# First norm of a hybrid block on one core: the weights as a scale of the evictions, two tiles turned by a diagonal, two turned plainly at another place

## The chip, the cores and the metric

The kernel runs on one core of a Trainium2 chip. The metric is the device time of one execution in microseconds, as the median of several runs. The core has five engines with queues of their own: PE (matrix products; its weight loads are listed as PEld), ACT (functions, with a scale and a bias per partition), DVE (element by element), POOL and SP. Data lie in 128 partitions; PE writes to PSUM banks of 128 x 512 f32 values, and ACT and DVE read them from there.

## The reference

512 tokens and 16 meta tokens in front of them (528 rows of 1024 values) pass a block: a norm over the row, a wide projection, a recurrent branch (convolution of 4 taps, two gates, a scan), a retention branch with four heads, their gated sum, and a feed-forward part with a convolution. The part that matters here is the first norm and the start of the recurrent branch:

```python
def rms_norm(x, g):
    x32 = x.astype(jnp.float32)
    y = x32 * lax.rsqrt(jnp.mean(x32 * x32, axis=-1, keepdims=True) + EPS)
    return (y * g.astype(jnp.float32)).astype(x.dtype)
...
h = jnp.concatenate([meta, x], axis=1)
xn = rms_norm(h, norm_mix_g[l])
z = xn @ w_in[l]
u_rnn, u_gate, q, k, v, g_ret, ga, gb = jnp.split(z, IN_SPLITS, axis=-1)
xr = causal_dwconv(u_rnn, rnn_conv_w[l], rnn_conv_b[l])
...
r = jax.nn.sigmoid(jnp.einsum('btni,nij->btnj', xb, w_a).reshape(bsz, t, D_RNN) + b_a)
i = jax.nn.sigmoid(jnp.einsum('btni,nij->btnj', xb, w_x).reshape(bsz, t, D_RNN) + b_x)
```

A row is divided by its root mean square, which is one number per token, and multiplied by a weight, which is one number per column.

## The kernel before

**Precision.** Every f32 operand of a product is split into a high and a low f16 part: ACT writes the high part (`split`, L91), DVE the rest (L92). A product of two operands takes three f16 products (high by high, high by low, low by high). The split normalized tokens are the tiles xh and xl, with the 1024 columns as 8 blocks of 128 partitions and the tokens along the free axis. Weights come by SP's queue into one of two raw buffers (`unit_load`, 1 MB or 0.5 MB a unit) and are split in steps into tiles wt; a raw buffer is free for the next load when DVE has done the last step of its unit.

**The first norm.** Tokens come as four tiles of 128 rows, two in each tile xin. For each tile ACT sums the squares (`rms_scale`, L320) and takes the root, DVE the reciprocal rs, and DVE multiplies the rows by rs and by the weights, which were read from memory into all 128 partitions (tile gmix, 512 KB, L402). PE turns the result by eight transposes into two PSUM banks (L411), and ACT and DVE split them into xh and xl, 512 columns at a time. The 16 meta tokens go a way of their own in the tile xmeta (L440 to L452). In between PE runs matmuls on zeros, `keep_warm` (L426), 18, 2, 5 and 6 of them.

**The first blocks.** The recurrent branch has ten blocks of 128 columns. The product of a block is done in two halves of tokens of 24 products each; the first half reads the meta tokens and tiles 0 and 1. `first_half` (L383) does the first halves of blocks 0, 1 and 2 as soon as these two tiles are split; tiles 2 and 3 are normed and turned meanwhile. Then the loop over the ten blocks starts: the second halves of blocks 0 to 2, from block 3 on whole blocks (48 products, L370); the convolution as a scaled copy on ACT (L537) and three taps on DVE (L539); the split of the result (tile xs); and three blocks later (LAG) the two gate products, with sigmoids on ACT (L556). `tick` emits weight steps of coming units between. The gate weights a and x are loaded into raw buffers by `load_gates` and split by `split_gates` (tiles gw), a behind the product of block 0, x behind that of block 2.

**Order.** From the first norm to the end of the recurrent branch, the orders of PE, ACT and DVE are those in which the program is written (`manual_schedule`); loads by `load` are kept in their written order on SP's queue. Each engine works in order: an instruction that waits holds those behind it.

Of the kernel before, what the change touches and what calls it, by code (L numbers as in the profile page):

```python
# [14 lines left out]
P = 128  # L15
T = 528
# [34 lines left out]
def hybrid_block_kernel(ctx, tc, x, meta, norm_mix_g, w_in, conv_w, conv_b, rg_a_w, rg_a_b,  # L51
# [44 lines left out]
    def load(dst, src):  # L96

        if last_load[0] is None:
            last_load[0] = nc.sync.dma_start(dst, src)
        else:  # L100
            with tc.issue_after(last_load[0].ins):
                last_load[0] = nc.sync.dma_start(dst, src)
# [7 lines left out]
    def unit(nk, ncol, parts, fast=False):  # L110
        units.append((nk, ncol, parts, fast))
        return len(units) - 1

    o_ur, o_ug, o_q, o_k, o_v, o_gr, o_ga, o_gb = 0, 1280, 2560, 3584, 4608, 6656, 8704, 9728
    u_ur = []
    for n in range(2):
        u_ur.append((unit(8, P, [(0, 0, kmaj(w_in, 0, 8, o_ur + P * n, P))]), 0))
    for i in range(1, 5):
        u = unit(8, 256, [(0, 0, kmaj(w_in, 0, 8, o_ur + 256 * i, 256))])
        u_ur += [(u, 0), (u, P)]  # L120
    u_ug = [unit(8, 256, [(0, 0, kmaj(w_in, 0, 8, o_ug + 256 * i, 256))]) for i in range(5)]
# [138 lines left out]
    def queue(new):  # L260
        steps.extend((len(loaded) - 1, run) for run in new)
# [52 lines left out]
    def pair(name):  # L314
        return [piece([P, 512], F32, f"{name}{a}") for a in range(2)]
# [79 lines left out]
    def token_rows(i):  # L395
        return xin[i // 2][:, i % 2]

    def first_rows(i, rs):
        xn_t[i] = pair("xn")
        for a in range(2):  # L400
            sl = slice(a * 512, (a + 1) * 512)
            nc.vector.scalar_tensor_tensor(xn_t[i][a], token_rows(i)[:, sl], rs, gmix[:, sl], op0=ALU.mult, op1=ALU.mult)  # L402

    def first_transpose(i, banks):
        xn = xn_t.pop(i)
        c0 = 3 + NM + P * i
        pvs = []
        for a in range(2):
            pv = banks[a].rearrange("p (b c) -> p b c", c=P)
            for k in range(4):  # L410
                nc.tensor.transpose(pv[:, k], xn[a][:, k * P:(k + 1) * P], ident)  # L411
            pvs.append(pv)

        def finish(*half):
            for a in half:
                sl = slice(4 * a, 4 * a + 4)
                split(xh[:, sl, c0:c0 + P], xl[:, sl, c0:c0 + P], pvs[a], S_XN)
        return finish

    warm = work.tile([P, 512], F16, name="warm", tag="w")  # L420
    nc.vector.memset(warm, 0.0)
# [12 lines left out]
    pmeta = acc("pmeta")[:, 0]
    xm, gm = xmeta[:, 0:P], xmeta[0:8, P:2 * P]
    first_rows(0, rms_scale(token_rows(0), P, "n"))
    finish0 = first_transpose(0, ptr_banks())
    first_rows(1, rms_scale(token_rows(1), P, "n"))
    ssm = small.tile([P, 4], F32, name="ssm")
    nc.scalar.activation(xmeta[:, 2 * P:3 * P], xm, AF.Square, accum_out=ssm[:, 0:1])  # L440
    nc.tensor.matmul(pmeta[:, 0:P], pick[0:8, 0:P], gm, start=True, stop=True)
    nc.tensor.matmul(pmeta[:, 2 * P:2 * P + 1], same[:, 0:P], ssm[:, 0:1], start=True, stop=True)
    finish0(0)
    finish0(1)
    keep_warm(2)
    pt1 = acc("pt1")
    finish1 = first_transpose(1, [pt1[:, 0], pt1[:, 1]])
    nc.scalar.activation(ssm[:, 1:2], pmeta[:, 2 * P:2 * P + 1], AF.Sqrt, scale=1.0 / D, bias=eps_t)
    nc.vector.reciprocal(ssm[:, 2:3], ssm[:, 1:2])
    nc.vector.scalar_tensor_tensor(xm, xm, ssm[:, 2:3], pmeta[:, 0:P], op0=ALU.mult, op1=ALU.mult)  # L450
    keep_warm(5)
    nc.tensor.transpose(pmeta[:, P:2 * P], xm, ident)  # L452
    keep_warm(6)
    def first_step():
        steps[done[0]][1]()
        done[0] += 1

    first_step()
    finish1(0)
    split(xh[:, :, 3:3 + NM], xl[:, :, 3:3 + NM], pmeta[:, P:2 * P].rearrange("p (t c) -> p c t", c=8), S_XN)  # L460
    first_step()
    finish1(1)
    first_rows(2, rms_scale(token_rows(2), P, "n"))
    first_half(0)
    for i in range(2):
        first_step()
    finish2 = first_transpose(2, ptr_banks())
    rs3 = rms_scale(token_rows(3), P, "n")
    finish2(0, 1)
    first_rows(3, rs3)  # L470
# [218 lines left out]
    nc.sync.dma_start(dec_meta, decay_t[:, :, T:].rearrange("h p c -> p h c"))  # L689
# [721 lines left out]
```

## Time and profile before

| | us |
|---|---|
| median of 3 runs (1078.16 to 1082.24) | 1078.28 |
| the profiled execution | 1080.82 |
| its span | 1079.1 |
| PE busy | 1059.0 |
| DVE busy | 839.4 |
| ACT busy | 568.2 |
| PE, first product that counts (L383) starts | 17.68 |
| PE, second half of block 0 starts | 28.68 |

The profile is one execution. Times in it count from the start of its span. A row of the timeline has the start, the busy time, the engine, the line, the operation, what it writes and reads, the shapes and the number of instructions; in brackets is the idle time of the engine before it and what ended it. A row of the chain of waits has start, length and what ran. A row of windows has the stretch, its length, the busy time and count of PE, PEld, DVE, ACT and POOL, then the granted clock of PE, the share of the DMA engines and GB/s. A DMA row has the queue, the count, the size and the time from issue to landing. Where a row has "x2" for one f32 product, these are its two passes.

### The profile page before, as it was taken

To read this page: it belongs to the slowest core of one execution; us is meant where nothing else is said; L and a number is where in the kernel's file an instruction comes from. 1 tells how busy PE (TensorE), PEld (TensorE's weight loads), DVE (VectorE), ACT (ScalarE), POOL (GpSimd) and SP (SyncE) were. 2 spreads that over 40 slices of the span, in tenths; PEclk is the share of its full clock that TensorE was granted. 3 is DMA by queue.
4 is the path that set the end of the run, shared out by engine and by line. 5 is a ranking of instruction groups with operands and counts; after the bars stand their busy time and mean duration, and the time that the engine had idled before them with its cause. 6 is when DMAs were issued, how large, how long until landed. Compare 5 with 4: busy or idle time off the path is not lost.

```text
span 1079.1 us, 20969 instructions
## 1 busy us (share of the span) xinstructions
PE 1059.0 (98%) x9045; PEld 856.6 (79%) x9045; DVE 839.4 (78%) x1220; ACT 568.2 (53%) x847; POOL 6.9 (1%) x20
## 2 busy tenths in 40 slices
PE   8999999999999999999999999999999999999997
PEld 5888888875684858888888885588888888888885
DVE  5875699998786969888697785478767776888875
ACT  6568963534564747566454453364544454454442
POOL 2000000000000000000000000000000000000000
PEclk9999999999999999999999999999999999999999
DMA  6423243431211311433333355053232323113322
GB/s 209 143 92 104 79 138 118 157 119 40 75 45 50 108 64 65 125 91 118 104 103 118 118 199 173 2 196 115 81 118 80 118 79 118 40 60 121 115 79 79
DMA packets 105957, 112.02 MB, mean 104 GB/s; under 512 B 3470, under 2 KB 97396, under 8 KB 105864
## 3 DMA queue, kind: packets, MB, share of 16 engines
q1 hardware_dynamic: 105432, 110.27, 31.1%
q8 instruction: 71, 1.16, 0.4%
q10 hardware_dynamic: 144, 0.26, 0.1%
q14 instruction: 22, 0.18, 0.1%
q0 software_dynamic: 288, 0.14, 0.0%
HBM read 108.57 MB, written 2.10 MB: 103 GB/s over the span
## 4 chain that ended last, share of the span: by engine, by line
PE 71%; DVE 17%; ACT 8%; issue 2%; DMA 2%; SPq 0%; ACTq 0%; DVEq 0%
PE ps L370 33%; PE P L1247 9%; PE pa L775 7%; DVE wt L92 4%; PE ps L838 4%; PE pm L370 4%; PE ps L1119 3%; PE ps L383 3%; PE pe L775 3%; ACT wt L91 2%; PE pb L775 2%; PE ps L860 1%; DVE rnn L574 1%; DVE raw L231 1%; DMA raw<-in_w_out 1%
## 5 line engine op out<-in xcount | busy, mean ns | idle before, releaser
L370 PEld LDWEIGHTS <-wt 128*128 128x128 f16 x4224 | 410.5, 97 | 63.7 <-DVE t L666 1.4
L92 DVE SCALAR_TENSOR_TENSOR wt<-raw,wt 128x1024 f16<-128x1024 f32 (+2 forms) x270 | 296.2, 1110 | 71.7 <-ACT wt L91 69.8
L91 ACT ACTIVATE wt<-raw 128x1024 f16<-128x1024 f32 (+2 forms) x270 | 256.1, 964 | 161.3 <-PE ps L370 28.3
L775 PEld LDWEIGHTS <-wt 128*128 128x128 f16 x2016 | 195.0, 97 | 36.0 <-issue 8.8
L370 PE MATMUL ps<-x2h,wt 128*128 128x258 f16 x1440 | 218.8, 273 | 0.0
L370 PE MATMUL ps<-xh,wt 128*128 128x257 f16 (+2 forms) x1056 | 163.8, 275 | 1.1 <-DVE t L666 1.1
L370 PE MATMUL ps<-x2l,wt 128*128 128x258 f16 x720 | 137.7, 272 | 0.0
L1204 DVE SCALAR_TENSOR_TENSOR cv<-ps,vt,cv 128x512 f32<-128x512 f32 x96 | 71.9, 748 | 54.5 <-ACT cv L1202 53.2
L370 PE MATMUL ps<-xl,wt 128*128 128x257 f16 (+2 forms) x528 | 102.2, 275 | 0.0
L1247 PE MATMUL P<-wt,act 128*128 128x256 f16 x792 | 88.3, 273 | 0.0
L1247 PEld LDWEIGHTS <-act 128*128 128x128 f16 x792 | 77.5, 98 | 9.0
L838 PE MATMUL ps<-wt,xh 128*128 128x512 f16 x256 | 76.4, 379 | 1.2 <-DVE v L92 1.0
L775 PE MATMUL pa<-xs,wt 128*128 128x257 f16 x576 | 71.6, 273 | 4.8 <-ACT kept L780 4.5
L1202 ACT ACTIVATE cv<-ps,vt,vt 128x512 f32<-128x512 f32 x48 | 37.1, 774 | 56.8 <-PE ps L370 52.2
L370 PE MATMUL pm<-oa,wt 128*128 128x257 f16 x480 | 55.4, 274 | 0.0
L838 PEld LDWEIGHTS <-xh 128*128 128x128 f16 x256 | 24.8, 98 | 30.9 <-issue 2.9
L838 PE MATMUL ps<-wt,xl 128*128 128x512 f16 x128 | 48.5, 379 | 0.0
L775 PE MATMUL pa<-ob,wt 128*128 128x257 f16 x384 | 45.7, 274 | 0.6 <-ACT last L780 0.5
L1119 PE MATMUL ps<-wt,mx 128*128 128x512 f16 x192 | 44.8, 379 | 0.5 <-DVE mx L92 0.5
L231 DVE TENSOR_TENSOR raw<-raw 128x1024 f32<-128x1024 f32 x35 | 42.7, 1220 | 0.6
L1119 PEld LDWEIGHTS <-mx 128*128 128x128 f16 x192 | 17.4, 98 | 19.2 <-DVE mx L92 1.0
L860 PE MATMUL ps<-sc,v 128*128 128x257 f16 (+4 forms) x384 | 32.1, 236 | 0.0
(253 smaller groups left out, 1278.1 us busy)
## 6 DMA issues: line engine op xcount, KB each, us to landing
raw<-in_w_in SPq DMA_DIRECT2D x41, 1024.0 KB, 4.9
raw<-in_w_up SPq DMA_DIRECT2D x24, 1024.0 KB, 5.0
raw<-in_w_down SPq DMA_DIRECT2D x48, 256.0 KB, 3.6
raw<-in_w_branch_ret SPq DMA_DIRECT2D x16, 512.0 KB, 4.0
raw<-in_w_branch_rnn SPq DMA_DIRECT2D x8, 640.0 KB, 4.2
raw<-in_w_out SPq DMA_DIRECT2D x4, 1024.0 KB, 4.9
xin<-in_x SPq DMA_DIRECT2D x4, 512.0 KB, 6.6
h<-in_x SPq DMA_DIRECT2D x4, 512.0 KB, 4.9
```

What stands on the lines that cost most here:

```text
L91: nc.scalar.activation(hi, src, AF.Copy, scale=s)
L92: nc.vector.scalar_tensor_tensor(lo, src, s, hi, op0=ALU.mult, op1=ALU.subtract)
L231: nc.vector.tensor_tensor(pair, pair, rv[:, :, right].rearrange("p (h k) c -> p h k c", h=2), op=ALU.add)
L370: nc.tensor.matmul(ps[:, hf, :n], w(aw, k, col, P), src(ax, k, c0, n), start=k == 0 and (aw, ax) == (0, 0), stop=k == nk - 1 and aw == 1)
L383: nc.tensor.matmul(ps[:, hf, :n], w(aw, k, col, P), src(ax, k, c0, n), start=k == 0 and (aw, ax) == (0, 0), stop=k == KD - 1 and aw == 1)
L775: nc.tensor.matmul(ps[:, :257], ws[k // 4](wf, aw, k % 4), src(xf_, ax, k), start=first and k == 0 and (aw, ax) == (0, 0), stop=k == last_ ...
L838: nc.tensor.matmul(pb, xf(ax, k, XF + j0, nb), w(aw, k % 4, 0, 512), start=i == 0, stop=i == 23)
L860: nc.tensor.matmul(ps[:, hf, s0 - lo_i:257], vt[b][:, va, d * P:(d + 1) * P], st[SCP[b][0]][:, sa, o:o + hi_i - s0], start=i == 0, stop=i ...
L1119: nc.tensor.matmul(ps[:, n], mx[k][:, a, c0:c0 + P], wo[k // 2](aw, k % 2, n * 512, 512), start=j == 0, stop=j == 23)
L1202: nc.scalar.activation(vv_, ps[:, :, 2:258], AF.Identity, scale=vt2[:, 96 + ch:97 + ch], bias=b_ff[:, ch:ch + 1])
L1204: nc.vector.scalar_tensor_tensor(vv_, ps[:, :, j:j + 256], vt2[:, 48 * j + ch:48 * j + ch + 1], vv_, op0=ALU.mult, op1=ALU.add)
L1247: nc.tensor.matmul(pd[:, 256 * tt:256 * tt + 256], t[:, ax, c0 + tt * P:c0 + tt * P + P], w(wf, aw, i), start=q % 6 == 0 and tt == 0 and i ...
```

## The change

1. **Weights as a scale.** The broadcast tile gmix goes. The 1024 weights come as 8 rows of 128 into xmeta (a load that was there for the meta tokens; now it is issued from ACT's queue), are turned by one small transpose and kept, times S_XN, as gs: one column of 128 values per block of columns. ACT and DVE multiply by a column of gs when they split, so each 128 x 512 eviction becomes four of 128 x 128.
2. **Tiles 0 and 1** are turned without being scaled first: `first_scale` makes a diagonal of the reciprocals, dg, and the turning is a product of the token rows with dg in f32 instead of a transpose of scaled rows.
3. **Tiles 2 and 3** are scaled by rs alone and transposed as before. Tile 3 goes into the free second halves of the banks of blocks 0 and 1, and stands behind the first half of block 2 instead of ahead of it.
4. **Loads.** The first two blocks' weights, two units of 128 columns, become one unit of 256, like the next, both loaded and split column by column (`column_unit`). The load of dec_meta leaves the head of SP's queue.
5. **Warming** is 15, 4 and 5 matmuls.
6. **Gates and steps.** Block 0 is split and the x gates are split earlier, behind blocks 0 and 1, and the weight steps of blocks 0 and 1 stand behind blocks 2 and 3.

```diff
-    for n in range(2):
-        u_ur.append((unit(8, P, [(0, 0, kmaj(w_in, 0, 8, o_ur + P * n, P))]), 0))
-    for i in range(1, 5):
+    for i in range(5):
...
+    def column_unit():
...
+        def fetch(c):
+            load(rv[:, :, c * P:c * P + P], ap[:, :, c * P:c * P + P])
...
+                split(tv[0], tv[1], rv[:, 4 * i:4 * i + 4, c * P:c * P + P], SW)
...
+        queue([step(i, c) for c in range(2) for i in range(2)])
...
-    gmix = wsp.tile([P, D], F32, name="gmix", tag="wt")
...
+    nc.scalar.dma_start(xmeta[0:8, P:2 * P], norm_mix_g.rearrange("(c f) -> c f", f=P))
     load(xin[0][:, 0], x2[0:P])
     load(xin[0][:, 1], x2[P:2 * P])
-    load(gmix, norm_mix_g.partition_broadcast(P))
     load(xmeta[:, 0:P], meta.rearrange("t (c f) -> (t c) f", f=P))
-    load(xmeta[0:8, P:2 * P], norm_mix_g.rearrange("(c f) -> c f", f=P))
...
+    def first_scale(i):
+        rs = rms_scale(token_rows(i), P, "n")
+        dg = piece([P, 512], F32, "dg")[:, 0:P]
+        nc.vector.tensor_scalar_mul(dg, ident, rs)
+        return dg
...
-            nc.vector.scalar_tensor_tensor(xn_t[i][a], token_rows(i)[:, sl], rs, gmix[:, sl], op0=ALU.mult, op1=ALU.mult)
+            nc.vector.tensor_scalar_mul(xn[a], token_rows(i)[:, 512 * a:512 * a + 512], rs)
...
+        def turn(a):
             for k in range(4):
-                nc.tensor.transpose(pv[:, k], xn[a][:, k * P:(k + 1) * P], ident)
+                c = 512 * a + k * P
+                if dg is None:
+                    nc.tensor.transpose(pvs[a][:, k], xn[a][:, k * P:k * P + P], ident)
+                else:
+                    nc.tensor.matmul(pvs[a][:, k], token_rows(i)[:, c:c + P], dg, start=True, stop=True)
+        def high(a):
+            for k in range(4):
+                g = gs[:, 4 * a + k:4 * a + k + 1]
+                nc.scalar.activation(xh[:, 4 * a + k, c0:c0 + P], pvs[a][:, k], AF.Copy, scale=g)
+        def low(a):
+            for k in range(4):
+                g = gs[:, 4 * a + k:4 * a + k + 1]
+                nc.vector.scalar_tensor_tensor(xl[:, 4 * a + k, c0:c0 + P], pvs[a][:, k], g,
+                                               xh[:, 4 * a + k, c0:c0 + P], op0=ALU.mult, op1=ALU.subtract)
...
-    keep_warm(18)
+    keep_warm(15)
...
+    nc.tensor.transpose(pmeta[:, 3 * P:3 * P + 8], gm, ident[0:8, 0:8])
+    nc.vector.tensor_scalar_mul(gs, pmeta[:, 3 * P:3 * P + 8], S_XN)
...
-    finish3 = first_transpose(3, ptr_banks())
     first_half(2)
...
+    turn3, high3, low3 = first_transpose(3, [early[i][:, 1] for i in range(2)], xn=xn3)
...
-            tick(2 if n in (6, 8) else 1)
+            tick(2 if n in (3, 6, 8) else 1)
...
-        if n < 2:
+        if n == 0:
+            conv_split(0)
+        if n == 1:
+            split_gates("x")
+        if n == 2:
             tick()
-        if n == 2:
-            conv_split(0)
-            split_gates("x")
...
-    nc.sync.dma_start(dec_meta, decay_t[:, :, T:].rearrange("h p c -> p h c"))
+    load(dec_meta, decay_t[:, :, T:].rearrange("h p c -> p h c"))
```

Three places show how the instructions move; lines are those of each kernel.

DVE from the first reciprocal, before (xn are the scaled rows, xin the token tiles):

```order
L324 RECIPROCAL rs<-sd 128x1
L402 SCALAR_TENSOR_TENSOR xn_154<-xin_110,rs,gmix 128x512
L402 SCALAR_TENSOR_TENSOR xn_155<-xin_110,rs,gmix 128x512
L324 RECIPROCAL rs<-sd 128x1
L402 SCALAR_TENSOR_TENSOR xn_175<-xin_110,rs,gmix 128x512
L402 SCALAR_TENSOR_TENSOR xn_176<-xin_110,rs,gmix 128x512
L92 SCALAR_TENSOR_TENSOR xl<-ptr,xh 128x4x128 x2
```

and now:

```order
L345 RECIPROCAL rs<-sd 128x1
L428 TENSOR_SCALAR dg<-ident,rs 128x128
L490 TENSOR_SCALAR gs<-pmeta 128x8
L345 RECIPROCAL rs<-sd 128x1
L428 TENSOR_SCALAR dg<-ident,rs 128x128
L461 SCALAR_TENSOR_TENSOR xl<-ptr,gs,xh 128x128 x8
```

The four scaled rows of 512 columns give way to two diagonals, and the two low parts of 512 columns to eight of 128.

PE at tile 3 (xn_287 and xn_288), before; first halves of blocks are the L383 rows:

```order
L411 MATMUL ptr<-ident,xn_287 128x128 x4
L411 MATMUL ptr<-ident,xn_288 128x128 x4
L383 LDWEIGHTS wt
L383 MATMUL ps<-xh,wt 128x267
L383 LDWEIGHTS wt
L383 MATMUL ps<-xl,wt 128x267
```

and now (xn_353 and xn_354; L406 is what L383 was, and these are the first products of block 0's second half):

```order
L449 MATMUL ps<-ident,xn_353 128x128 x4
L449 MATMUL ps<-ident,xn_354 128x128 x4
L556 MATMUL ptv<-ident,v_401 128x128
L557 MATMUL ptv<-ident,v_402 128x128
L558 MATMUL ptv<-ident,v_402 128x24
L406 LDWEIGHTS wt
L406 MATMUL ps<-xh,wt 128x267
```

Before, 24 products of block 2 stood between tile 3's transposes and their first reader; now three small transposes stand there.

ACT from the first bias of the convolution (rnn) to the first sigmoids (gi), before:

```order
L537 ACTIVATE rnn<-ps,vt_93,cwr 128x528 x2
L91 ACTIVATE wt<-raw 128x1024
L537 ACTIVATE rnn<-ps,vt_93,cwr 128x528
L91 ACTIVATE xs<-rnn 128x528
L91 ACTIVATE gw<-raw 128x512 x2
L91 ACTIVATE gw<-raw 128x256
L91 ACTIVATE xs<-rnn 128x528 x2
L91 ACTIVATE wt<-raw 128x1024
L556 ACT_TABLE_LOAD
L556 ACTIVATE rnn<-ps,vt_93 128x528
L556 ACTIVATE gi<-ps,vt_93 128x528
```

and now:

```order
L600 ACTIVATE rnn<-ps,vt_93,cwr 128x528
L91 ACTIVATE xs<-rnn 128x528
L600 ACTIVATE rnn<-ps,vt_93,cwr 128x528
L91 ACTIVATE gw<-raw 128x512 x2
L91 ACTIVATE gw<-raw 128x256
L600 ACTIVATE rnn<-ps,vt_93,cwr 128x528
L91 ACTIVATE wt<-raw 128x1024
L91 ACTIVATE xs<-rnn 128x528 x2
L91 ACTIVATE wt<-raw 128x1024 x2
L619 ACT_TABLE_LOAD
L619 ACTIVATE rnn<-ps,vt_93 128x528
L619 ACTIVATE gi<-ps,vt_93 128x528
```

The split of block 0 and the x gates move ahead of block 2's bias, and a third weight step (wt), of the unit after, stands ahead of the table load.

More of the change, by code (lines that the diff above doesn't have):

```diff
@@ L210, in unit_load, with step, run @@
         return [step(i, c) for i in range(2) for c in range(cuts)]
+    def column_unit():
+        _, ncol, parts, _ = units[len(loaded)]
+        raw = wraw.tile([P, 2048], F32, name="raw")
+        rv = raw.rearrange("p (k c) -> p k c", c=ncol)
+        ap = parts[0][2]
+        tiles = []
+        def fetch(c):
+            load(rv[:, :, c * P:c * P + P], ap[:, :, c * P:c * P + P])
+        def step(i, c):
+            def run():
+                if c == 0:
+                    tiles.append(wsp.tile([P, 2, 1024], F16, name="wt"))
+                tv = [tiles[i][:, a].rearrange("p (k c) -> p k c", c=ncol)[:, :, c * P:c * P + P] for a in range(2)]
+                split(tv[0], tv[1], rv[:, 4 * i:4 * i + 4, c * P:c * P + P], SW)
+            return run
+        loaded.append(len(loaded))
+        wviews.append(lambda a, k, c0, m: tiles[k // 4][:, a, k % 4 * ncol + c0:k % 4 * ncol + c0 + m])
+        queue([step(i, c) for c in range(2) for i in range(2)])
+        return fetch
     def fast_steps(rv, bk, bc):
@@ L345, in hybrid_block_kernel @@
         xin.append(xt)
+    nc.scalar.dma_start(xmeta[0:8, P:2 * P], norm_mix_g.rearrange("(c f) -> c f", f=P))
     load(xin[0][:, 0], x2[0:P])
     load(xin[0][:, 1], x2[P:2 * P])
-    load(gmix, norm_mix_g.partition_broadcast(P))
     load(xmeta[:, 0:P], meta.rearrange("t (c f) -> (t c) f", f=P))
-    load(xmeta[0:8, P:2 * P], norm_mix_g.rearrange("(c f) -> c f", f=P))
-    queue(unit_load())
+    fetch = column_unit()
+    fetch(0)
     load(xin[1][:, 0], x2[2 * P:3 * P])
-    queue(unit_load())
+    fetch(1)
     load(xin[1][:, 1], x2[3 * P:4 * P])
-    xn_t = {}
+    fetch = column_unit()
+    fetch(0)
+    fetch(1)
     SPLIT = ((0, 0), (0, 1), (1, 0))
@@ L396, in token_rows, with first_rows, first_transpose @@
         return xin[i // 2][:, i % 2]
-    def first_rows(i, rs):
-        xn_t[i] = pair("xn")
+    gs = const.tile([P, KD], F32, name="gs")
+    def first_scale(i):
[3 more added lines that the diff above has]
+        return dg
+    def first_rows(i):
+        rs = rms_scale(token_rows(i), P, "n")
+        xn = pair("xn")
         for a in range(2):
[L401 to L405, printed above, removed]
+            nc.vector.tensor_scalar_mul(xn[a], token_rows(i)[:, 512 * a:512 * a + 512], rs)
+        return xn
+    def first_transpose(i, banks, dg=None, xn=None):
         c0 = 3 + NM + P * i
-        pvs = []
-        for a in range(2):
-            pv = banks[a].rearrange("p (b c) -> p b c", c=P)
+        pvs = [b.rearrange("p (b c) -> p b c", c=P) for b in banks]
+        def turn(a):
             for k in range(4):
[L411 to L418, printed above, removed]
+                c = 512 * a + k * P
[12 more added lines that the diff above has]
+                                               xh[:, 4 * a + k, c0:c0 + P], op0=ALU.mult, op1=ALU.subtract)
+        return turn, high, low
     warm = work.tile([P, 512], F16, name="warm", tag="w")
@@ L431, in ptr_banks @@
         return [bank("ptr") for _ in range(2)]
-    keep_warm(18)
[L434 to L453, printed above, removed]
     def first_step():
@@ L456, in first_step @@
         done[0] += 1
+    keep_warm(15)
+    pmeta = acc("pmeta")[:, 0]
+    xm, gm = xmeta[:, 0:P], xmeta[0:8, P:2 * P]
+    ssm = small.tile([P, 4], F32, name="ssm")
+    dg0 = first_scale(0)
+    turn0, high0, low0 = first_transpose(0, ptr_banks(), dg=dg0)
+    nc.tensor.transpose(pmeta[:, 3 * P:3 * P + 8], gm, ident[0:8, 0:8])
+    nc.vector.tensor_scalar_mul(gs, pmeta[:, 3 * P:3 * P + 8], S_XN)
+    turn0(0)
+    turn0(1)
+    dg1 = first_scale(1)
+    pt1 = acc("pt1")
+    turn1, high1, low1 = first_transpose(1, [pt1[:, 0], pt1[:, 1]], dg=dg1)
@@ new lines, in hybrid_block_kernel @@
+    high0(0)
+    nc.scalar.activation(xmeta[:, 2 * P:3 * P], xm, AF.Square, accum_out=ssm[:, 0:1])
+    high0(1)
+    nc.tensor.matmul(pmeta[:, 0:P], pick[0:8, 0:P], gm, start=True, stop=True)
+    turn1(0)
+    nc.tensor.matmul(pmeta[:, 2 * P:2 * P + 1], same[:, 0:P], ssm[:, 0:1], start=True, stop=True)
+    turn1(1)
+    nc.scalar.activation(ssm[:, 1:2], pmeta[:, 2 * P:2 * P + 1], AF.Sqrt, scale=1.0 / D, bias=eps_t)
+    low0(0)
+    low0(1)
+    nc.vector.reciprocal(ssm[:, 2:3], ssm[:, 1:2])
@@ L458, in hybrid_block_kernel @@
+    nc.vector.scalar_tensor_tensor(xm, xm, ssm[:, 2:3], pmeta[:, 0:P], op0=ALU.mult, op1=ALU.mult)
+    keep_warm(4)
+    nc.tensor.transpose(pmeta[:, P:2 * P], xm, ident)
+    keep_warm(5)
     first_step()
-    finish1(0)
+    high1(0)
     split(xh[:, :, 3:3 + NM], xl[:, :, 3:3 + NM], pmeta[:, P:2 * P].rearrange("p (t c) -> p c t", c=8), S_XN)
+    low1(0)
     first_step()
-    finish1(1)
-    first_rows(2, rms_scale(token_rows(2), P, "n"))
+    high1(1)
+    low1(1)
     first_half(0)
-    for i in range(2):
-        first_step()
@@ L467, in hybrid_block_kernel @@
[L467 to L470, printed above, removed]
-    first_half(1)
-    queue(unit_load(2))
-    for i in range(4):
-        first_step()
-    finish3 = first_transpose(3, ptr_banks())
-    first_half(2)
-    finish3(0, 1)
+    first_step()
+    first_step()
+    xn2 = first_rows(2)
+    first_half(1)
+    turn2, high2, low2 = first_transpose(2, ptr_banks(), xn=xn2)
+    turn2(0)
+    turn2(1)
+    first_step()
@@ L480, in hybrid_block_kernel @@
+    first_step()
+    first_half(2)
+    xn3 = first_rows(3)
+    for a in range(2):
+        high2(a)
+        low2(a)
+    first_step()
+    turn3, high3, low3 = first_transpose(3, [early[i][:, 1] for i in range(2)], xn=xn3)
+    turn3(0)
+    turn3(1)
+    for a in range(2):
+        high3(a)
+        low3(a)
+    first_step()
     v1 = work.tile([P, T], F32, name="v1", tag="w")
```

## The prediction

> **What bounds the kernel now.** I read the page's busy shares first, then what PE waited for, then the chain of waits in order of time.
>
> ```profile
> span 1079.1 us, 20969 instructions
> PE 1059.0 (98%) x9045; PEld 856.6 (79%) x9045; DVE 839.4 (78%) x1220; ACT 568.2 (53%) x847; POOL 6.9 (1%) x20
> ...
> PE ptr L411 <- DVE xn L402: 2.7, 1, 2.7
> ...
> 2.32 7.05 DMA gmix<-in_norm_mix_g
> ...
> 10.40 1.23 PE ptr L411 x8
> ...
> 28.68 8.37 PE ps L383 x72
> 37.05 47.73 PE ps L370 x414
> ...
> 84.81 0.71 ACT rnn L556
> ```
>
> PE is busy 98% of the span, so an edit of the first 30 us can win or lose only the time in which PE there does something other than products that count. In the chain the first 9.4 us belong to the broadcast weights gmix: they land at 9.37, PE has waited 2.7 us, and the first transpose starts at 10.40. From 28.68 PE has products without a gap up to 84.78, and what follows (ACT at 84.81) is released by it. Past the recurrent blocks the engines' orders are the same in both kernels, so what PE gains or loses up to there is carried to the end. The sum therefore has three stations: the first product that counts, the second half of block 0 (28.68), and the waits behind it.
>
> **Start: the wait for gmix goes.**
>
> ```profile
> 0.81 0.43 SPq L689 DMA_DIRECT2D dec_meta<-decay  x1
> 1.31 0.49 SPq L99 DMA_DIRECT2D xin<-in_x  x1
> 1.50 6.16 PE L426 MATMUL ps<-warm 128*128 128x512 f16 x18 [1.50 <-DVE warm L421]
> 2.10 0.20 ACT L287 ACTIVATE sq_t<-eps_t 128x1 f32<-128x1 f32 x1
> 5.18 1.06 ACT L320 ACTIVATE junk<-xin 128x1024 f16<-128x1024 f32 x1 [2.87 <-DMA xin<-in_x]
> ...
> 5.75 1.42 PEld L426 LDWEIGHTS <-warm 128*128 128x128 f16 x7 [0.28 <-issue]
> ...
> 6.69 0.16 DVE L324 RECIPROCAL rs<-sd 128x1 f32<-128x1 f32 x1 [5.24 <-ACT sd L322]
> ...
> 28.72 0.29 DVE L496 COPY vt<-ptv 128x128 f32<-128x128 f32 x1
> 28.92 0.30 DVE L497 TENSOR_SCALAR vt<-ptv 128x144 f32<-128x144 f32 x1
> ```
>
> Tile 0 is squared 3.87 us after its issue (1.31 to 5.18). With dec_meta off the head of SP's queue it is issued at 0.81, so the square starts at 4.68, the reciprocal 1.51 later (6.69 less 5.18), at 6.19, and a diagonal of 128x128, at most the 0.30 of the nearest row, is there by 6.65. PE comes later: warming ended at 7.66, its last seven loads were 0.21 apart, so 15 of them end at 7.02. The weights are transposed ahead of tile 0, about 0.15 for one transpose (8 in 1.23 above), so the turning starts at 7.2 instead of 10.40: **-3.2**.
>
> That needs the 4 KB of weights, now on ACT's queue behind the table and sq_t and so issued near 2.3, to land by 7.0. The trace has no load from that queue. From below, 3.87 as for tile 0 costs nothing; from above stands a small load through POOL's queue under the same traffic:
>
> ```profile
> v<-in_rnn_conv_w POOLq DMA_DIRECT2D x1, 20.0 KB, 5.5
> ```
>
> It would land at 7.8, a loss of 0.8. I take no loss, since tile 0 is the nearer row: a queue whose engine does nothing else at that time. The issue on ACT has its cover in the 2.87 us for which ACT waits for tile 0. gmix leaves SP's queue, which brings meta, the units and tiles 2 and 3 forward, all of them ahead of their use. The issue of dec_meta (0.43) now lies between unit loads; its reader, the scores, runs past 230 us: nothing.
>
> **The turning by a diagonal** puts true f32 products, two passes each, in the place of the transposes of tiles 0 and 1.
>
> ```profile
> 11.55 0.29 PEld L441 LDWEIGHTS pmeta<-xmeta,pick 8*128 8x128 f32 x2 [0.17 <-issue]
> 11.55 0.48 PE L441 MATMUL pmeta<-xmeta,pick 8*128 8x128 f32 x2
> 11.97 0.38 PE L442 MATMUL pmeta<-ssm,same 128*128 128x1 f32 x2
> ...
> 12.21 0.65 PE L426 MATMUL ps<-warm 128*128 128x512 f16 x2
> 12.66 1.91 PE L411 MATMUL pt<-ident,xn 128*128 128x128 f32 x8
> ...
> 14.36 2.07 PE L426 MATMUL ps<-warm 128*128 128x512 f16 x5
> ...
> 16.38 1.46 PE L426 MATMUL ps<-warm 128*128 128x512 f16 x6
> ...
> 17.68 0.28 PE L383 MATMUL ps<-xh,wt 128*128 128x267 f16 x1
> ...
> 299.03 1.11 PE L875 MATMUL ps<-ssum,ones 128*128 128x257 f32 x4 [0.22 <-DVE ssum L868]
> ```
>
> No row has a full f32 product of 128 columns. A pass is bounded below by its weight load: L441's two, 0.18 each, lie within 0.29, so 0.11 apart. From above stands L441 itself, two passes in 0.42 (to 11.97), 0.21 each. Four passes of 257 columns at L875 take 0.95 (two matmuls, up to the next product at 299.98), which is 0.12 for 128 columns; I take this, because it alone is a run of passes with 128 rows. 16 passes make 1.9 us a tile. Tile 0's transposes took 1.15 (10.40 to 11.55), **+0.75**; tile 1's 1.70 (12.66 to 14.36), **+0.2**. The warming between, 2, 5 and 6 matmuls, took 0.45, 1.91 and 1.30 (to 17.68), 3.66 in all; now 9 at 0.21 are 1.9: **-1.75**. pick and same, 0.66 up to 12.21, become four passes, 0.48: **-0.2**. With the start this sums to -4.2: the first product that counts at 13.5.
>
> **Scaling in the eviction** makes four pieces of 128x128 of each 128x512 one, on ACT for the high part and on DVE for the low one.
>
> ```profile
> 16.58 0.28 ACT L91 ACTIVATE xh<-pmeta 128x128 f16<-128x128 f32 x1 [1.37 <-PE pmeta L452]
> 16.76 0.62 ACT L91 ACTIVATE wt<-raw 128x512 f16<-128x512 f32 x1
> 17.27 0.59 ACT L91 ACTIVATE xh<-pt 128x512 f16<-128x512 f32 x1
> ...
> L402 DVE SCALAR_TENSOR_TENSOR xn<-xin,rs,gmix 128x512 f32<-128x512 f32 x8 | 5.6, 746 | 2.7 <-DMA gmix<-in_norm_mix_g 2.6
> ```
>
> On ACT a piece costs between 0.18, one start to the next (16.58 to 16.76), and its duration 0.28; I take 0.20, so four take 0.8 where one took 0.51. On DVE it is between 0.20 (28.72 to 28.92) and 0.29; I take 0.24. Tiles 0 and meta hide behind the turning and warming, tile 1's second half doesn't: ACT starts it only when DVE has done the low pieces of the first. Meta's transpose stands five warmings ahead of 13.5, at about 12.3. Then ACT 0.28, meta's low part on DVE 0.25, four low pieces 0.96, four high ones 0.8, the first low one 0.3, and some 0.4 for the hand-overs: 15.3. PE has 12 products first (0.115 each, 47.73 for 414) and asks for it at 14.9: **+0.4**, the bounds 0.1 and 1.0. So block 0's first half ends 3.8 early. The scaled rows of tiles 2 and 3, at the old 0.75 apiece or less, hide behind the halves of blocks 0 and 1.
>
> Tile 3 loses its cover. Its eight transposes stood ahead of the third half (24 products, 2.77 us); now they stand behind it, and what follows is the second half of block 0, which reads their result. PE would ask for it at 28.68-3.8 = 24.9. The third half ends at 23.2, the first four transposes are out at 23.9, their high pieces at 24.8, and the first low weights may be loaded only behind the fourth low piece: 25.9. **+1.0** (0.8 to 1.7), which leaves **-2.8** at this station.
>
> **Gates ahead** is where the next wait arises. Times here count from the start of block 0's second half (28.68 before, 25.9 now).
>
> ```profile
> 30.94 0.37 SPq L102 DMA_DIRECT2D raw<-in_w_in  x1
> ...
> 35.76 1.06 ACT L91 ACTIVATE wt<-raw 128x1024 f16<-128x1024 f32 x1 [0.64 <-DMA raw<-in_w_in]
> ...
> 41.48 1.62 DVE L92 SCALAR_TENSOR_TENSOR gw<-raw,gw 128x512 f16<-128x512 f32 x3
> ...
> 42.59 1.28 ACT L556 ACT_TABLE_LOAD   x1
> ...
> 45.06 0.79 ACT L537 ACTIVATE rnn<-ps,vt,cwr 128x528 f32<-128x528 f32 x1
> 46.01 2.37 DVE L539 SCALAR_TENSOR_TENSOR rnn<-ps,cwr,rnn 128x528 f32<-128x528 f32 x3
> ...
> raw<-in_rg_x_w SPq DMA_DIRECT2D x1, 640.0 KB, 4.1
> ```
>
> Block 5 takes the bank that block 3's taps free. They ended at 48.4, 19.7 on; PE asks after three halves, blocks 3 and 4 whole and two sets of gates, 72, 96 and 24 products, 192x0.115 = 22.1. The slack was 2.4. Now the split of block 0 and the x gates stand ahead of block 2's taps, and a third weight step ahead of the first sigmoid. Walked by these rows: bias and taps of block 0 with two copies to 6.5; its high part to 7.15; block 1's bias 7.9 and taps 10.2; the x gates on DVE 1.55 more, 11.75. Only that frees the buffer of the next unit: issue to use is 4.8 (30.94 to 35.76), 16.55. ACT works in order, so behind this step (0.95) queue the table (1.28), two sigmoids (1.2) and block 3's bias (0.8): 20.8; the taps end at 23.2, 23.4 with some 0.2 for hand-overs. PE waits **1.3** at block 5; 0.7 if the gate loads' 4.1 to landing held here too, 1.8 if the walk lies half a microsecond low. Behind it nothing new is late, since from there each block asks the same work of all three as before.
>
> Sum: -2.8+1.3 = **-1.5**. The profiled execution's 1080.82 (1.7 around its span) would be 1079.3; it lies 2.5 above the median of the runs, so I forecast 1078.28-1.5 = 1076.8.
>
> **The clock.**
>
> ```profile
> 12.90:13.60 0.70, 0.70 (x5) 0.70 (x4) 0.70 (x3) 0.27 (x1) 0.00 (x0) 0.50 1.04 402
> ...
> 16.30:17.50 1.20, 1.20 (x8) 0.60 (x7) 0.38 (x2) 0.92 (x3) 0.00 (x0) 1.00 0.00 0
> ```
>
> Behind PE's gap of 2.7 us and the transposes the granted clock fell to 0.50, and is whole again by 16.3. I reckon with full clock, since PE has no gap now. [...]
>
> **Rivals.**
> 1. Block 5 finds its bank free, because DVE or the transfer is quicker than walked: -2.8, 1075.5. For it, the slack was 2.4; against, the buffer's release stands in one order on DVE. 0.22.
> 2. Slower than before: a pass of 128 columns costs L441's 0.21, load and stream not overlapping. 32 passes by 0.09 more are 2.9: +1.4, 1079.7. It decides from 0.17 a pass, where the 1.5 are gone. For it L441, against it L875. 0.13.
> 3. Half clock from 12.6 to 16.0 as before: the last four warmings end 0.85 late, the products behind go at half pace for 1.7 us, the wait of 0.4 is swallowed: +1.2, 1078.0. 0.12.
> 4. The change doesn't remove the wait but hands it to the small load: +0.8, 1077.6. 0.10.
>
> **How the numbers follow.** The forecast has 0.43. The range, 1075.0 to 1080.3, goes from rival 1 with the low bounds of the pieces (0.5 less) to rival 2 with half of their high ones (0.6 more), and leaves out about 0.2. A measurement of this kernel tells 0.5%, 5.4 us, from no change, and no case alone comes to that. Rivals 2, 3 and 4 together with the high bounds do (+2.9+1.2+0.8+1.8-1.5 = 5.2): slower 0.04. Faster would need the first product at 10, when tile 0 is only just turned: 0.04. No change 0.92.
>
> **What would show it.** Right: the first f32 product near 7.2, 16 passes in 1.9, the first counted product near 13.5, block 0's second half near 26, and one wait of PE of about 1.3 near 48. Wrong: a gap of PE up to 7.9 (rival 4), passes 0.2 apart (2), 0.50 in the windows from 12 to 16 (3), no gap near 48 (1), or, against the whole sum, a shift behind 85 us that differs from the one at 50.

## The result

| | us |
|---|---|
| before, median of 14 runs (1078.13 to 1082.24) | 1078.39 |
| changed, median of 14 runs (1080.07 to 1082.60) | 1080.67 |
| ratio | 1.0019, 95% interval 1.0011 to 1.0027 |
| the changed kernel's profiled execution | 1081.30 |
| its span | 1079.5 |

The change makes the kernel 2.3 us slower, inside the half per cent that was called no change, but clear of its interval, 3.9 above the forecast of 1076.8 and 0.4 above the upper end of the range.

The page of the changed kernel, span and busy time:

```profile
span 1079.5 us, 21039 instructions
PE 1058.6 (98%) x9055; PEld 857.2 (79%) x9055; DVE 840.3 (78%) x1243; ACT 571.6 (53%) x871; POOL 6.9 (1%) x20
```

PE's timeline in the changed kernel (start, busy time, line, what it writes and reads, count; in brackets the idle time before and what ended it). It shows the head, the first product that counts (14.54), and the three places at which PE waits from there on:

```profile
1.50 6.27 PE L472 MATMUL ps<-warm 128*128 128x512 f16 x15 [1.50 <-DVE warm L467]
...
7.86 2.05 PE L451 MATMUL ptr<-dg,xin 128*128 128x128 f32 x16
9.84 0.48 PE L499 MATMUL pmeta<-xmeta,pick 8*128 8x128 f32 x2
...
12.36 1.03 PE L472 MATMUL ps<-warm 128*128 128x512 f16 x4
...
13.46 1.24 PE L472 MATMUL ps<-warm 128*128 128x512 f16 x5
14.54 0.28 PE L406 MATMUL ps<-xh,wt 128*128 128x267 f16 x1
...
16.91 0.27 PE L406 MATMUL ps<-xl,wt 128*128 128x267 f16 x1 [0.71 <-DVE xl L461]
...
27.55 0.29 PE L406 MATMUL ps<-xh,wt 128*128 128x267 f16 x1 [1.58 <-DVE xl L461]
...
50.97 0.40 PE L393 MATMUL ps<-xh,wt 128*128 128x267 f16 x2 [1.15 <-DVE rnn L602]
```

Each kind of step is there as forecast: f32 products 0.124 apart (16 in 1.98, up to 9.84), a short wait at tile 1's second half, a wait at tile 3, a wait at block 5. From the first product that counts to the release of ACT near 85 (shown below) it takes 70.54; in the profile of before it took 67.13. The difference, 3.4, is about the sum of the three waits (0.71, 1.58 and 1.15). In the chain of waits the last one reads so, and the run of products behind it releases ACT at 85.08 (84.81 in the first profile of before):

```profile
39.19 4.96 DMA raw<-in_w_in
44.17 1.06 ACT wt L91
45.24 1.28 ACT L619
...
50.97 34.08 PE ps L393 x294
85.08 0.71 ACT rnn L619
```

So profile against profile the kernel lost 0.27 up to there and 0.4 in the span, where the sum had a gain of 1.5. But 0.4 is not 2.3. The rest lies in the kernel before: in the execution that its profile caught.

### The profile page after: what moved, and what is told of

The parts are those of the page before. It is cut to its first block, busy times and chain, and to the rows that moved or that the text cites. A ratio compares the mean times of both kernels' runs of the same rounds, so it can differ in the third digit from the quotient of the medians.

```text
span 1079.5 us, 21039 instructions
## 1 busy us (share of the span) xinstructions
PE 1058.6 (98%) x9055; PEld 857.2 (79%) x9055; DVE 840.3 (78%) x1243; ACT 571.6 (53%) x871; POOL 6.9 (1%) x20
## 4 chain that ended last, share of the span: by engine, by line
PE 72%; DVE 16%; ACT 9%; issue 2%; DMA 1%; ACTq 0%; DVEq 0%
PE ps L393 31%; PE P L1311 9%; PE pa L839 8%; PE ps L902 4%; PE pm L393 4%; DVE wt L92 4%; PE pe L839 3%; PE ps L1183 3%; ACT wt L91 2%; PE pb L839 2%; PE ps L406 2%; PE ps L924 1%; DVE rnn L637 1%; DVE raw L253 1%; DVE rnn L602 1%
## 5 line engine op out<-in xcount | busy, mean ns | idle before, releaser
L393 PEld LDWEIGHTS <-wt 128*128 128x128 f16 x4224 | 410.4, 97 | 65.1 <-DVE rnn L602 1.4
L839 PEld LDWEIGHTS <-wt 128*128 128x128 f16 x2016 | 195.1, 97 | 36.0 <-issue 8.8
L406 PEld LDWEIGHTS <-wt 128*128 128x128 f16 x288 | 27.9, 97 | 7.0 <-DVE xl L461 1.7
```

The source lines that it names most:

```text
L393: nc.tensor.matmul(ps[:, hf, :n], w(aw, k, col, P), src(ax, k, c0, n), start=k == 0 and (aw, ax) == (0, 0), stop=k == nk - 1 and aw == 1)
L406: nc.tensor.matmul(ps[:, hf, :n], w(aw, k, col, P), src(ax, k, c0, n), start=k == 0 and (aw, ax) == (0, 0), stop=k == KD - 1 and aw == 1)
L839: nc.tensor.matmul(ps[:, :257], ws[k // 4](wf, aw, k % 4), src(xf_, ax, k), start=first and k == 0 and (aw, ax) == (0, 0), stop=k == last_ ...
```

## The experiments

The theory under test (A): the profile on which the sum was made was no usual execution of the kernel before, and the losses are three separate waits, each with a cause that can be removed alone. Times of before beside the runs lay at 1078.42 to 1078.55 (medians of 21 to 33 runs). Behind each median stands in brackets the ratio to before with its 95% interval; it is not the quotient of the two medians. The intervals of single repairs overlap with that of the changed kernel, so for each of them it is the trace that shows what became of its wait.

**Before, a second profile.** No edit.

> The kernel before, unchanged, for a second profile. Theory A: the half clock from 12.6 to 16.0 in the first profile of before is no property of the kernel but of that execution, which lay 2.5 us above the median; an execution near the median (span about 1076.7) has the clock whole from 10 to 17, its first product that counts starts at 15.0 to 16.0 instead of 17.68, and the rest of the span is as long as in the first profile. Rival B: the early stage is the same in each execution (17.7), and the 2.5 us lie elsewhere, behind 85 us.

The profiled execution took 1078.37, span 1076.7; median of 8 runs 1078.47. Its PE timeline:

```profile
9.46 1.23 PE L411 MATMUL ptr<-ident,xn 128*128 128x128 f32 x8 [1.46 <-DVE xn L402]
...
11.70 1.04 PE L411 MATMUL pt<-ident,xn 128*128 128x128 f32 x8
12.57 1.24 PE L426 MATMUL ps<-warm 128*128 128x512 f16 x5
13.65 0.27 PE L452 MATMUL pmeta<-ident,xmeta 128*128 128x128 f32 x1
13.76 1.46 PE L426 MATMUL ps<-warm 128*128 128x512 f16 x6
15.06 0.28 PE L383 MATMUL ps<-xh,wt 128*128 128x267 f16 x1
...
25.99 0.29 PE L383 MATMUL ps<-xh,wt 128*128 128x267 f16 x1
```

and the window in which the first profile had the clock at 0.50 (granted clock is the third number from the end):

```profile
12.90:13.60 0.70, 0.70 (x5) 0.34 (x3) 0.70 (x2) 0.47 (x1) 0.00 (x0) 1.00 1.02 410
```

The chain of waits has the transfer of gmix, which had taken 7.05:

```profile
2.31 6.11 DMA gmix<-in_norm_mix_g
```

gmix came 0.9 earlier, the clock stayed whole, and five warmings took 1.08 instead of 1.91. The turning starts 0.94 earlier and what stands between it and the first product that counts takes 1.68 less. The first product that counts starts at 15.06 instead of 17.68; these 2.6 are still there at block 0's second half (25.99 against 28.61) and, but for 0.2, in the span (1076.7 against 1079.1). Theory A holds, B falls: all of the 2.5 by which the first profile lay above the median was lost ahead of 17.68, at the very place that the change rebuilds. Two things stay open. No run tests whether the longer gap of PE behind the late gmix (2.73 instead of 1.46) brought the half clock on. And 3 of the 14 runs of before lie at 1080.0 or above; with two profiles it isn't shown whether the others of them lost it at this place too.

**Part 6 undone as written.**

```diff
-            tick(2 if n in (3, 6, 8) else 1)
+            tick(2 if n in (6, 8) else 1)
...
-        if n == 0:
-            conv_split(0)
-        if n == 1:
-            split_gates("x")
-        if n == 2:
-            tick()
+        if n < 2:
+            tick()
+        if n == 2:
+            conv_split(0)
+            split_gates("x")
```

> The changed kernel with part 6 undone: the splits of block 0 and the x gates and the weight steps stand where they stood before. Theory A: PE's wait of 1.15 us at block 5 goes and nothing takes its place: 1080.67 - 1.15 = 1079.5. Rival: the wait is only handed on, to the sigmoids or to a later unit's load: 1080.4 to 1080.9.

1087.48 (1.0082, 1.0068 to 1.0096). The rival had the wait handed on to a unit's load, but at 1080.9 at most. ACT meets a weight step behind block 0 already and stands there for a transfer, PE waits for the gates, and the clock falls on top (ACT, PE, and the window behind the gap):

```profile
38.29 1.06 ACT L91 ACTIVATE wt<-raw 128x1024 f16<-128x1024 f32 x1 [7.78 <-DMA raw<-in_w_in]
```

```profile
46.97 2.36 PE L393 MATMUL ps<-xs,gw 128*128 128x264 f16 x10 [4.35 <-DVE xs L92]
```

```profile
47.00:50.00 3.00, 3.00 (x14) 2.00 (x14) 2.69 (x5) 0.92 (x1) 0.00 (x0) 0.50 0.62 190
```

The same lines of code no longer give the order of before: with one unit of two columns in the place of two units, the first `tick` emits a step where it emitted none before. So this run says nothing yet on the order.

**Tile 3 turned inside the third half, alone and with the edit above.** The function given to `first_half` is called behind 12 of its 24 products.

```diff
+    xn3 = first_rows(3)
+    turn3, high3, low3 = first_transpose(3, [early[i][:, 1] for i in range(2)], xn=xn3)
-    first_half(2)
-    xn3 = first_rows(3)
+    first_half(2, lambda: (turn3(0), turn3(1)))
...
-    turn3, high3, low3 = first_transpose(3, [early[i][:, 1] for i in range(2)], xn=xn3)
-    turn3(0)
-    turn3(1)
```

> The changed kernel with tile 3's eight transposes in the middle of block 2's first half (behind 12 of its 24 products) instead of behind it; nothing else moved. Theory A: its high pieces start on ACT near 24.3 instead of 25.2, PE's gap ahead of block 0's second half falls from 1.58 to 0.5 to 0.8, and the gap at block 5 stays 1.1 to 1.2: 1079.6 to 1079.9. Rival: the chain behind (bias, taps, x gates, load) does not come forward with it, the gap at block 5 grows by what the first one loses: 1080.7.

1079.68 (1.0007, 0.9998 to 1.0016), 1.0 below the changed kernel, as theory A had it. The gap ahead of block 0's second half went from 1.58 to 0.61; that at block 5 stayed, 0.15 longer:

```profile
1.51 4.74 PE L474 MATMUL ps<-warm 128*128 128x512 f16 x15 [1.51 <-DVE warm L469]
...
25.08 0.29 PE L408 MATMUL ps<-xh,wt 128*128 128x267 f16 x1 [0.61 <-DVE xl L463]
...
48.65 0.40 PE L393 MATMUL ps<-xh,wt 128*128 128x267 f16 x2 [1.30 <-DVE rnn L602]
```

> Both of the edits above in the changed kernel. Theory A: they add up, 1.15 + 0.9: 1078.6, the time of before (1078.4) within 0.5. Rival: one cause behind both waits, the gain is that of the larger alone: 1079.5 or more.

1086.99 (1.0069, 1.0056 to 1.0082): the fault of the undone part 6 covers the gain, so the question of adding up stayed open here.

**One weight step a block later.**

```diff
-            tick(2 if n in (3, 6, 8) else 1)
+            tick(2 if n in (4, 6, 8) else 1)
```

> The changed kernel with one weight step moved: the second of the two steps ahead of the first sigmoids stands one block later; all else as in the change. Theory A (the step that waits for its transfer holds ACT): the step's 1.10 of waiting and 1.06 of work leave the way of the sigmoids and of block 3's bias, so PE's gap of 1.15 at block 5 goes: 1080.67 - 1.15 = 1079.5. Rival: with x gates and block 0 split ahead of block 2's taps, DVE is what is late; the gap stays at 0.8 or more: 1080.3 to 1080.7.

1079.38 (1.0006, 0.9997 to 1.0015), 1.3 below the changed kernel; its profile has no wait of PE between 27 and 85 us any more. What PE waited for up to 90 us, beside the start of the warming:

```profile
PE ps L406 <- DVE xl L461: 2.3, 2, 1.6
```

From the first product that counts to ACT's release near 85 it takes 69.22 instead of 70.54. So theory A holds: the step ahead of the sigmoids, with its wait for the transfer and its work (the run doesn't part the two), was the whole cause of the wait at block 5.

**A bank of its own for tile 1's second half.** In the change both halves of tile 1 lie in one tile of two banks, and the program then orders ACT's reads of the second half behind DVE's of the first.

```diff
-    turn1, high1, low1 = first_transpose(1, [pt1[:, 0], pt1[:, 1]], dg=dg1)
...
     high0(1)
+    low0(0)
+    low0(1)
+    turn1, high1, low1 = first_transpose(1, [pt1[:, 0], bank("ptr")], dg=dg1)
```

> The changed kernel with the second half of tile 1 in a bank tile of its own (one that tile 0 has left) instead of the second half of the tile that holds the first; orders of ACT, DVE and PE as in the change. Theory A: ACT's high pieces of that half no longer wait for DVE's low pieces of the first half (0.88 us of waiting), they start near 14.5 where they started at 15.3 in the profile, PE's gap of 0.71 in block 0's first half falls to 0.1 to 0.3, and all behind comes 0.5 earlier: 1080.1. Rival: DVE's own four pieces, 0.28 apart, are the bound; the gap stays near 0.7: 1080.7.

1079.72 (1.0009, 1.0000 to 1.0018), 0.95 below the changed kernel. ACT at this place in the changed kernel:

```profile
15.33 1.14 ACT L456 ACTIVATE xh<-pt,gs 128x128 f16<-128x128 f32 x4 [0.88 <-DVE xl L461]
```

and with the bank of its own, with no wait in front:

```profile
14.09 1.14 ACT L456 ACTIVATE xh<-ptr,gs 128x128 f16<-128x128 f32 x4
```

In PE's first half 0.18 of the wait is left (15.54 to 15.95 for two products that take 0.23), and block 0's second half starts 12.30 behind the first product that counts instead of 13.01. The wait at block 5 grows to 1.4, so that at 85 half a microsecond is left of it (70.06 instead of 70.54): theory A's 0.5. The rest of the 0.95 lies ahead of the first product that counts and in the spread of the runs; the fastest of the two kernels, 1079.46 and 1080.07, are 0.6 apart.

**gmix earlier, in the kernel before.**

```diff
+    load(gmix, norm_mix_g.partition_broadcast(P))
     load(xin[0][:, 1], x2[P:2 * P])
-    load(gmix, norm_mix_g.partition_broadcast(P))
```

> The kernel before with one load moved: gmix stands ahead of tile 1's rows on SP's queue. Both theories hold that before's first transpose waits for gmix. Theory A: it lands 1.2 to 1.5 earlier, near 7.2, the first transpose starts near 8.2 instead of 9.46, tile 1 is still there in time, and the kernel gains about 1.0: 1077.4. Rival: tile 1 (landing 1.3 later) and the work on DVE take the place of that wait, and the first product that counts stays near 15: 1078.4.

1078.40 (0.9999, 0.9990 to 1.0008). The rival holds:

```profile
8.22 1.23 PE L411 MATMUL ptr<-ident,xn 128*128 128x128 f32 x8 [0.90 <-DVE xn L402]
...
10.38 0.38 PE L442 MATMUL pmeta<-ssm,same 128*128 128x1 f32 x2 [0.52 <-ACT xmeta L440]
...
14.98 0.28 PE L383 MATMUL ps<-xh,wt 128*128 128x267 f16 x1
```

The turning starts 1.24 earlier and the first product that counts 0.08. Tile 1, now behind gmix, took the place of the wait: ACT squares it at 8.56 instead of 6.88, having waited 2.20 for its rows; the run does not say what gmix earlier would be worth with tile 1 not later.

**The order of before, truly restored** (the first weight step behind block 1's bias, as in before).

```diff
-            tick(2 if n in (3, 6, 8) else 1)
+            tick(2 if n in (6, 8) else 1)
...
-        if n == 0:
-            conv_split(0)
         if n == 1:
-            split_gates("x")
+            tick()
         if n == 2:
-            tick()
+            conv_split(0)
+            split_gates("x")
```

> The changed kernel with the splits of block 0 and of the x gates and the weight steps in the very order that ACT and DVE have in the kernel before (the run called gates_back had the first weight step one block earlier than before). Theory C: the changed kernel issues the x gates' load and the next unit's load later against block 0's second half (1.6 and 3.7 behind its start in gates_back, where before has -1.5 and 2.3), so the old order would hold ACT at its weight step until some 11 to 12 us behind that start, and the gates of block 0 come 2 to 4 us late: 1082 to 1084. Rival: only the misplaced step made gates_back slow, and the old order is as good as with the step moved later: 1079.4.

1082.78 (1.0040, 1.0027 to 1.0052): theory C. The loads on SP's queue, first in the second profile of before (block 0's second half at 25.99), then here (at 26.54):

```profile
24.58 0.37 SPq L102 DMA_DIRECT2D raw<-in_rg_x_w  x1
28.33 0.37 SPq L102 DMA_DIRECT2D raw<-in_w_in  x1
```

```profile
28.14 0.37 SPq L102 DMA_DIRECT2D raw<-in_rg_x_w  x1
30.25 0.37 SPq L102 DMA_DIRECT2D raw<-in_w_in  x1
```

```profile
37.59 1.06 ACT L91 ACTIVATE wt<-raw 128x1024 f16<-128x1024 f32 x1 [4.54 <-DMA raw<-in_w_in]
...
42.85 2.36 PE L393 MATMUL ps<-xs,gw 128*128 128x264 f16 x10 [2.09 <-DVE xs L92]
```

The x gates are issued 1.6 behind the station instead of 1.4 ahead of it, because the raw buffer that they use is freed by the last early weight step, which the change puts behind tile 3's pieces (it ends on DVE at 28.11, and the load is issued at 28.14). The next unit is issued 2.1 behind them instead of 3.75, and takes 7.3 to its use instead of 4.8. ACT stands 4.54 for it. PE's wait of 2.09 is not the whole cost: behind it the granted clock is 0.50 for 3.41 us (42.81 to 46.22, in which the ten products above take 2.36), which is another 1.7 lost. In the changed kernel the clock stays whole behind its wait of 1.15 (1.00 in the window from 49 to 54). So part 6 of the change is no loss against the old order: the new place of tile 3 and of the weight steps made the loads late, and part 6 buys a part of that back, most of it as clock.

**Fewer warmings.**

```diff
-    keep_warm(15)
+    keep_warm(9)
```

> The changed kernel with 9 warming matmuls at the head instead of 15. Theory A (the clock rises at a time that differs between executions, 4.2 to 7.3 us in the profiles so far, and 15 warmings at half pace hold the turning till 6.2 to 7.9): 9 end at 5.4 even at half pace, the first f32 product then waits for the diagonal alone and starts at 6.3 to 6.5 in every execution; median 0.6 lower, 1080.1, and the spread of its runs (1080.07 to 1082.6) shrinks to 0.6. Rival: with less work ahead the turning itself runs at half pace until the clock rises, 16 passes by up to 0.1: 1080.7 or more.

1080.58 (1.0021, 1.0012 to 1.0030), no gain, and its runs lie in two groups, six from 1080.01 to 1080.58 and five from 1081.68 to 1082.47. The profile fell in the second group:

```profile
1.50 4.02 PE L472 MATMUL ps<-warm 128*128 128x512 f16 x9 [1.50 <-DVE warm L467]
5.46 0.27 PE L489 MATMUL pmeta<-ident,xmeta 8*128 8x8 f32 x1
6.75 3.79 PE L451 MATMUL ptr<-dg,xin 128*128 128x128 f32 x16 [1.02 <-DVE dg L428]
```

The turning starts 1.1 earlier than in the changed kernel's profile, but at half pace: 16 passes in 3.71 (to 10.46) instead of 1.98. The rival was right for such executions. The others have the time that theory A gives, but no profile shows their turning.

**The repairs together.** First: tile 3 inside the third half, the later step, the bank of its own, and 12 warmings.

> The changed kernel with tile 3 turned inside block 2's first half, the later weight step, tile 1's second bank, and 12 warming matmuls instead of 15. Theory A: the losses add up and can be taken back one by one: 1080.67 - 1.0 - 1.15 - 0.5 - 0.6 (three warmings, 0.2 to 0.4 each, as far as the clock has risen) = 1077.4, below before's 1078.4. Rival: the early start is worth nothing, since what follows is bound by ACT and DVE: 1078.4 or more.

1077.28 (0.9980, 0.9971 to 0.9989): theory A, the losses add up. Then also one weight step moved behind tile 3's pieces:

```diff
         high2(a)
         low2(a)
-    first_step()
     for a in range(2):
         high3(a)
         low3(a)
     first_step()
+    first_step()
```

> The best of the kernels above with one weight step moved from between the scaled pieces of tile 2 and tile 3 to behind those of tile 3. Theory A: the gap of 0.61 ahead of block 0's second half is that step's 0.5 on ACT and 0.6 on DVE; it falls to 0.0 to 0.2: 1077.28 - 0.5 = 1076.8. Rival: the weights of block 3 or the x gates' load, which comes later with the step, make a new wait: 1077.3 or more.

1076.95 (0.9985, 0.9976 to 0.9994). Both beat both kernels, by 1.3 to 1.5 us against before; between the two the runs do not decide. The second one's PE timeline:

```profile
6.70 2.05 PE L453 MATMUL ptr<-dg,xin 128*128 128x128 f32 x16 [0.24 <-DVE dg L430]
...
13.39 0.28 PE L408 MATMUL ps<-xh,wt 128*128 128x267 f16 x1
...
24.33 0.29 PE L408 MATMUL ps<-xh,wt 128*128 128x267 f16 x1 [0.20 <-DVE xl L463]
```

From the first product that counts to block 0's second half it takes 10.94, as the kernel before (10.93 in both of its profiles); the changed kernel took 13.01. Up to ACT's release near 85 the profiles give, in us:

| | first product that counts | ACT released | between |
|---|---|---|---|
| before, 2nd profile | 15.06 | 82.19 | 67.13 |
| changed | 14.54 | 85.08 | 70.54 |
| weight step later | 13.27 | 82.49 | 69.22 |
| tile 1's own bank | 14.28 | 84.34 | 70.06 |
| tile 3 inside | 13.03 | 82.76 | 69.73 |
| the three, 12 warmings | 13.54 | 81.09 | 67.55 |
| and one step moved | 13.39 | 80.53 | 67.14 |

The early start of the change is real, and with its waits removed it comes through to the end.

## Why the prediction was wrong

**The step that failed** is the last one: "it lies 2.5 above the median of the runs, so I forecast 1078.28-1.5 = 1076.8". It takes the 2.5 for something that lies around the stages of the sum. It lay inside them: of the -4.2 at the first station, 2.6 were the late gmix and the half clock of that one execution. Against the second profile of before the same forecast of the changed kernel, 13.5, is a gain of 1.6 only, and the whole sum is -1.5+2.5 = +1.0, a time of 1079.4: slower than before. In the prediction's terms: the turning starts 2.3 earlier than in the usual execution and not 3.2, tile 1's products cost 1.0 more than its transposes and not 0.2 (0.87 there, 1.70 in the first profile), and the warmings save 0.9 and not 1.75. What then still lies between 1079.4 and 1080.67 are terms of the right kind and too small a size, below.

The stations, in us from the start (by the timeline; the prediction's 28.68 is the chain's time for the product at 28.61):

| | before, 1st profile | before, 2nd profile | forecast | changed |
|---|---|---|---|---|
| turning starts | 10.40 | 9.46 | 7.2 | 7.86 |
| first product that counts | 17.68 | 15.06 | 13.5 | 14.54 |
| block 0, second half | 28.61 | 25.99 | 25.9 | 27.55 |
| ACT released near 85 | 84.81 | 82.19 | 83.3 | 85.08 |

**Start: the wait for gmix goes.** It went, and the small load was no bound (rival 4): it is issued at 0.98, not near 2.3, and its transpose runs at 5.46 with 9 warmings. But "its last seven loads were 0.21 apart, so 15 of them end at 7.02" took the moment at which the clock rises for a property of the program. The same 15 took 6.27 here, 4.74 in the run with tile 3 inside the third half. In before the wait for gmix swallowed that; now the start hangs on it. In the profile this was 0.66 of the sum.

**The turning by a diagonal.** 16 passes in 1.98 where 1.9 was forecast, 0.1 more; rival 2 (0.21 a pass) is out. The rest of the head, tile 1, the meta rows and nine warmings, came out 0.3 longer than summed, in pieces of 0.15 at most.

**Scaling in the eviction.** Right in kind, too small in size. On ACT the four pieces of 128 columns take 1.14 and on DVE 1.13, 0.26 from start to start on both, not 0.20 and 0.24, and the last of them lasts 0.38 and 0.34. The nearest row (0.18 from one start to the next) was of two different instructions. In the chain of the changed kernel:

```profile
25.19 1.15 ACT xh L456 x4
```

The two waits were forecast as 0.4 and 1.0. Between the two stations the changed kernel takes 2.1 more than before, against 1.4. The experiments on these places took back 1.0 (tile 3 inside the third half), 0.7 (the bank) and, with the step moved, 0.4 (0.61 to 0.20 in the gap).

**Gates ahead.** The walk held closely. Counted from block 0's second half, the third step could start at 16.62 (forecast 16.55), the taps of block 3 end at 23.4 (23.2 to 23.4), PE waits 1.15 (1.3). Moving that one step later removed the wait, as the walk says. Rival 1 is out.

What the walk did not see is why part 6 stands there: it priced the new order against the old one with the loads of before, and never asked what the new loads would do to the old order. With them the old order is 2.1 us slower than the change (1082.78 against 1080.67), and 3.4 slower than the new order with its step moved (1079.38); in its profile 1.7 of that is the half clock behind the wait.

**The clock.** Rival 3 did not occur: the window from 12.9 to 13.6 has the clock at 1.00 in the changed kernel. But it is at 1.00 there in the second profile of before as well, with transposes ahead of it, so no run here tells what the f32 products in their place did to the clock. One sum of the prediction falls short: 5.2 for rivals 2, 3 and 4 together is below the 5.4 that it needed, so the 0.04 for slower had no case behind it.

Together: the baseline cost 2.4, the sizes 1.8 (1.06 at the start, 0.7 in the waits), and the changed kernel's profile lies 0.6 above its own median: 2.4+1.8-0.6 = 3.6 of the 3.9. Of the other 0.3, 0.2 was lost behind 85 us in the changed kernel's profile, and 0.1 lies between the two medians of before, 1078.28 and 1078.39.

## What to carry to other kernels

When the profiled execution is not at the median, find the place where it lost the difference before any term is taken from it; where the change rebuilds that very place, the loss is counted as a gain unless it is taken out first, and a second profile of the kernel before is then worth more than any term of the sum. An eviction cut into four pieces cost more than a quarter for each here (1.14 on ACT in place of 0.59), and two engines that read halves of one PSUM tile were put in order by the program (ACT waited 0.88 for DVE, and not at all with a bank of its own for the second half): give each half a tile of its own. When several edits go together, price each against the others' state: here the old order of splits, which had no wait in the kernel before, was 2.1 us worse than the new one behind the later loads, and most of that, 1.7 by its profile, was the half clock behind its wait.

## What the runs showed of the hardware that was not expected

**The start of the full clock.** Warmings run 0.43 apart at first and 0.21 from some moment on; by the clock records of the traces this moment was 5.79 and 6.46 in the two profiles of before, 7.32 in the changed kernel and 4.24 with tile 3 inside the third half, with the first matmul at 1.50 or 1.51 in all of them. (The view by windows counts 1.00 ahead of the first change on record, so the pace there is read from the warmings: their weight loads are 0.43 apart up to 5.75 in the first profile of before, up to 6.18 in the second and up to 7.03 in the changed kernel.) So the moment lies 0.67 apart in two executions of one kernel, and 3.1 apart in two kernels with the same 15 warmings ahead. What sets it is not shown.

**Fewer warmings and a gap behind them.** With 9 warmings and 1.0 us idle behind them the recorded clock rose at 10.8, 3.5 later than the latest of the others. The two groups of that kernel's times, 1.8 apart, fit the half-paced turning (1.73 more); the profile shows it for one execution only, and no run parts the gap from the chance of the moment.

**The clock behind a gap.** Once the clock was whole, gaps of PE of up to 1.6 (1.58 in the changed kernel, 1.00 in the window from 26 to 29) left it whole in these profiles; in or behind those of 2.73 (first profile of before), 2.09 (the old order restored) and 4.35 (part 6 undone) it was 0.50 for 3.41, 3.41 and 6.83 us. No run here varies the gap alone.

**One late transfer.** In two executions, of the last kernel above and of the one with tile 3 inside the third half, a weight load far behind the change took 6.89 and 6.35 (chain of waits, the last kernel):

```profile
633.13 6.89 DMA raw<-in_w_out
```

In the first profile of before it is 4.85. PE waits 0.8 and 0.9 behind it there, and not in that profile. These executions lay 1.5 and 0.8 above the median of their kernel, so this is probably a part of the spread that no edit here touches.
